# A hybrid decoder block on one core: attention units at a shorter lane period, scan-order outputs, the attention norm applied to its outputs, a paced lane for the up operands, and down loads inside the up stage

## The chip, the cores and the metric

One core of a Trainium2 chip runs the whole block. The metric is the device time of one execution in microseconds; the kernel before takes 2269.36 us (median of 3 runs, 2268.54 to 2271.99). In the text, PE is TensorE (matmuls; PEld its weight loads), DVE is VectorE, ACT is ScalarE, POOL is GpSimd and SP is SyncE, whose queue issues most DMAs. An engine executes its own instructions in order; between engines and DMAs, semaphores say what is ready.

## The reference

512 tokens and 16 learned meta tokens, width 2048, all in float32. A state-space mixer and stick-breaking attention share one input projection and one output projection; a gated MLP with a causal convolution follows.

```python
hn = rmsnorm(h, norm_mix_g)
proj = hn @ w_in                                  # 2048 -> 1024 (u) + 3 * 1024 (q, k, v)
u = proj[..., :1024]; q, k, v = split(proj[..., 1024:], 3)
y_ssm = s5_mixer(u, ...)                          # 64 groups: diagonal complex scan over time,
                                                  # gelu, then y * sigmoid(y @ w_glu + b_glu)
y_attn = stick_breaking_attention(q, k, v)        # 16 heads of 64
mixed = concat([rmsnorm(y_ssm, g_ssm_out), rmsnorm(y_attn, g_attn_out)])
h = h + mixed @ w_out
hn = rmsnorm(h, norm_ffn_g)
gate, val = split(causal_depthwise_conv(hn @ w_up, conv_w, conv_b), 2)      # 5632 each
h = h + (silu(gate) * val) @ w_down
out = rmsnorm(h, norm_final_g)[:, 16:]

# stick breaking, per head:
log_keep = where(kpos < qpos, log_sigmoid(-z), 0)
w = where(kpos < qpos, exp(log_sigmoid(z) + cumsum_from_the_right(log_keep) - log_keep), 0)
y = w @ v
```

## The kernel before

Everything is kept transposed: features on the 128 partitions, the 528 (later 514) positions along the free axis. A float32 product is three matmuls: each operand is split into a high part, rounded to the matmul's format (a cast on ACT), and the low rest (a subtraction on DVE), and `mm3` (L317 to L319) adds high x high, high x low and low x high into one PSUM bank. Weights are split the same way as they stream in: `fetch` (L188, L195) issues the load on SP into one of three raw buffers, L239 casts on ACT (tiles `wh`), `sub` (L114) makes the rest on DVE (`wl`), about two blocks ahead of their use. The helpers `mul`, `add` and `sub` have the lines L108, L111 and L114, ACT's `act` L102.

`dense` runs one output tile of 128 features: for each block of 8 k-tiles and each half of the positions 24 matmuls, then the evacuation of the half's bank. Banks come from three pools: three `d`, three `z` (lanes), two `y`. While both lanes exist, `dbank` takes two of every five banks from `y`.

Work that isn't dense runs in lanes, Python generators that are advanced by the stream of dense matmuls. `pulse` adds 1.4 ns per column of each k-step to a credit, and each time the credit reaches `period` one lane step is written into the program at that place. So the order is fixed when the program is built. The scan lane comes first (period 1600), for eight chunks of 128 channels: `ssm_prep` builds a chunk's tables, `ssm_main` loads the chunk from `udram` (L711), multiplies, scans and stores to `ydram`. Then the attention lane (period `PERATT`), four units of four heads: a unit loads k, q, v (`s<-qkv`, L832), splits them, transposes v (L871, L874), and then puts out 12 items, one every two steps. Each item passes stage a (scores on PE, L914 to L930, exponentials and logarithm on ACT), stage a2 (suffix sums on DVE, L952 to L955), stage b (transposes L982, exponential) and stage c (times v, L1028 and, for the last 16 queries, L997), 2, 4 and 6 steps after a. `hold` stops the lanes, `drain` runs what is left of them without dense work in between.

The stages: three u tiles together (`banks`, six banks, emptied at the first L108 operations after the norm factor, L361 to L377), five more u tiles, 24 tiles of k, v and q, eight gate tiles (`w_glu`, lanes held), the output projection's 16 tiles over the state-space half (`out_part(y2, ...)`), `drain`, its 16 tiles over the attention half (`out_part(ya, ...)`), the up stage, the down stage, the final norm.

The state-space outputs come back from `ydram` with time split as four phases of 132; `ready_y` puts them into the order of time while splitting them (L1181 on ACT, L114 on DVE). The attention half's products are multiplied by the norm factor when they leave the bank, added to h on POOL, squared on ACT for the next norm, stored (`hres`) and scaled by the up stage's gain (`x_scaled`, L1297).

The up stage multiplies by a Strassen-like scheme: seven products (`PROD`) per pair of blocks, whose operands are sums and differences of the halves of `xg[p]` and `xg[p + 8]`. `x_part` makes one operand and splits it: sum on DVE, cast on ACT (L1318), rest on DVE (L114). For p = 0 to 4 (`EARLY`) all seven are made after the tile that completes the pair, for p = 5 to 7 in the first up block. `gated` computes the convolution, silu and product of one block in `later` steps inside the next block and stores it (`fact`); the down stage loads these again and splits them (`load_f`, `split_f`, L396), the first six after the up stage's end.

## Time and profile before

| | |
|---|---|
| median of 3 runs | 2269.36 us (2268.54 to 2271.99) |
| profiled execution | 2271.95 us, span 2270.2 us |
| mean granted TensorE clock | 0.979 |
| loads and stores | 335 MB at a mean of 148 GB/s |

The profile page gives, for each engine, busy time, share of the span and count of instructions. A row of waits reads: engine, tile and line that waited, `<-` what ended the wait, then total us, times and the longest. A row of groups reads: line, engine, operation, tiles out `<-` in, shapes, count, then busy us, mean ns of one, then the idle time of that engine ahead of them. Tile names are those of the program without numbers (`d`, `z`, `y` banks; `s` the common pool of 67 tiles; `at` attention scores; `rstd` a norm factor).

The stages in the profile, from the start: opening u tiles to 53 us; u tiles to 116; k, v, q to 524; gate to 573; output projection's state-space half to about 712, then the drain, and from about 730 its attention half; up stage 850 to 1756; down stage to 2257; final norm.

### The profile page before, as it was taken

How to read it: one execution, taken by the hardware profiler on the slowest of the kernel's cores; microseconds unless marked ns; L12 is line 12 of the kernel's file. 1: busy time of each engine (PE TensorE's matmuls, PEld its weight loads, DVE VectorE, ACT ScalarE, POOL GpSimd, SP SyncE). 2: the span in 40 equal slices, each digit the busy share in tenths (PEclk: the TensorE clock that was granted, in tenths of full speed). 3: DMA queues.
4: the chain of work that ended last, by engine and by line, in shares of the span. 5: the costliest groups of instructions: out<-in, count | busy, mean ns of one | idle time of the engine just before them, and what ended most of it. 6: DMA issues, size and time to landing. Idle time of an engine off the chain costs nothing.

```text
span 2270.2 us, 39806 instructions
## 1 busy us (share of the span) xinstructions
PE 2189.7 (96%) x16196; PEld 2071.2 (91%) x16196; DVE 1576.9 (69%) x2385; ACT 1045.9 (46%) x1668; POOL 251.7 (11%) x370
## 2 busy tenths in 40 slices
PE   7999999999998889999999999999999999999997
PEld 7999998998898888999999999999999788888887
DVE  7877776666777658777887778877787544444464
ACT  5154453565665445555455554555544222222235
POOL 0000000001221350101111011111110000000004
PEclk9999999999999998999999999999999999999999
DMA  5323234242333245777777777777775533333342
GB/s 210 112 93 105 95 99 137 95 123 80 117 123 101 91 144 150 195 194 200 195 195 192 195 201 194 195 195 192 201 194 159 202 122 121 116 119 118 112 148 75
DMA packets 118808, 335.11 MB, mean 148 GB/s; under 512 B 13025, under 2 KB 25697, under 8 KB 118625
## 3 DMA queue, kind: packets, MB, share of 16 engines
q1 hardware_dynamic: 100288, 269.56, 36.6%
q0 software_dynamic: 17472, 61.89, 13.2%
q8 instruction: 127, 2.08, 0.4%
q10 hardware_dynamic: 864, 1.11, 0.2%
q14 instruction: 57, 0.46, 0.1%
HBM read 300.23 MB, written 32.28 MB: 146 GB/s over the span
## 4 chain that ended last, share of the span: by engine, by line
PE 83%; DVE 7%; ACT 4%; issue 2%; DMA 2%; POOL 1%; SPq 0%; DVEq 0%; ACTq 0%; POOLq 0%
PE d L318 20%; PE d L317 19%; PE d L319 19%; PE z L318 4%; PE z L317 4%; PE z L319 4%; PE y L318 3%; PE y L317 3%; PE y L319 3%; DVE s L108 2%; DVE s L114 2%; DVE wl L114 1%; DMA s<-udram 1%; PE z L930 1%; ACT wh L239 1%
## 5 line engine op out<-in xcount | busy, mean ns | idle before, releaser
L317 PE MATMUL d<-s,wh 128*128 128x258 f32 (+4 forms) x3376 | 1047.0, 310 | 35.4 <-DVE s L108 17.0
L318 PE MATMUL d<-s,wh 128*128 128x258 f32 (+4 forms) x3376 | 1042.7, 309 | 7.2 <-DVE s L114 4.4
L319 PE MATMUL d<-s,wl 128*128 128x258 f32 (+4 forms) x3376 | 1036.1, 307 | 0.0
L317 PEld LDWEIGHTS d<-s,wh 128*128 128x128 f32 x3376 | 647.5, 192 | 67.3 <-DVE s L108 13.2
L318 PEld LDWEIGHTS d<-s,wh 128*128 128x128 f32 x3376 | 649.7, 192 | 39.5 <-DVE s L114 8.9
L319 PEld LDWEIGHTS d<-s,wl 128*128 128x128 f32 x3376 | 650.7, 193 | 27.7 <-DVE wl L114 0.2
L239 ACT CAST wh<-wr 128x1024 fp32r<-128x1024 f32 (+2 forms) x209 | 197.5, 945 | 420.5 <-PE d L318 327.0
L114 DVE TENSOR_TENSOR wl<-wr,wh 128x1024 fp32r<-128x1024 f32 (+2 forms) x209 | 235.5, 1127 | 106.8 <-ACT wh L239 106.5
L111 DVE TENSOR_TENSOR s<-s,d 128x512 f32<-128x512 f32 (+1 forms) x144 | 90.5, 629 | 261.6 <-PE d L319 256.5
L317 PE MATMUL z<-s,wh 128*128 128x258 f32 (+1 forms) x752 | 214.9, 286 | 2.4 <-ACT s L1318 2.4
L318 PE MATMUL z<-s,wh 128*128 128x258 f32 (+1 forms) x752 | 216.1, 287 | 0.0
L319 PE MATMUL z<-s,wl 128*128 128x258 f32 (+1 forms) x752 | 213.0, 283 | 0.0
L111 POOL TENSOR_TENSOR s<-s,s 128x514 f32<-128x514 f32 (+1 forms) x89 | 108.4, 1218 | 769.7 <-ACT s L102 653.3
L317 PE MATMUL y<-s,wh 128*128 128x258 f32 (+1 forms) x640 | 183.0, 286 | 0.0
L318 PE MATMUL y<-s,wh 128*128 128x258 f32 (+1 forms) x640 | 182.5, 285 | 0.0
L319 PE MATMUL y<-s,wl 128*128 128x258 f32 (+1 forms) x640 | 182.1, 285 | 0.0
L114 DVE TENSOR_TENSOR wl<-wu,wh 128x1024 fp32r<-128x1024 f32 x132 | 162.1, 1228 | 1.8 <-ACT wh L239 1.3
L239 ACT CAST wh<-wu 128x1024 fp32r<-128x1024 f32 x132 | 138.9, 1052 | 34.2 <-ACT s L102 32.6
L317 PEld LDWEIGHTS z<-s,wh 128*128 128x128 f32 x752 | 143.1, 190 | 3.3 <-ACT s L1318 3.2
L319 PEld LDWEIGHTS z<-s,wl 128*128 128x128 f32 x752 | 144.6, 192 | 0.0
L318 PEld LDWEIGHTS z<-s,wh 128*128 128x128 f32 x752 | 143.8, 191 | 0.6 <-DVE s L114 0.5
L114 DVE TENSOR_TENSOR wl<-wu_s,wh 128x1024 fp32r<-128x1024 f32 x88 | 108.3, 1230 | 38.6 <-ACT wh L239 38.6
(222 smaller groups left out, 2903.6 us busy)
## 6 DMA issues: line engine op xcount, KB each, us to landing
wu<-w_up SPq DMA_DIRECT2D x132, 512.0 KB, 5.1
wu_s<-w_up SPq DMA_DIRECT2D x88, 512.0 KB, 4.6
wu_s<-w_up POOLq DMA_DIRECT2D x88, 512.0 KB, 6.8
wr<-w_down SPq DMA_DIRECT2D x96, 384.0 KB, 3.0
wr<-w_in SPq DMA_DIRECT2D x63, 512.0 KB, 4.1
wr<-w_out SPq DMA_DIRECT2D x32, 512.0 KB, 3.9
fact<-s POOLq DMA_DIRECT2D x44, 256.0 KB, 2.7
s<-fact SPq DMA_DIRECT2D x44, 256.0 KB, 3.4
```

What stands on the lines that cost most here:

```text
L108: e.tensor_tensor(out, a, b, op=ALU.mult)
L111: e.tensor_tensor(out, a, b, op=ALU.add)
L114: e.tensor_tensor(out, a, b, op=ALU.subtract)
L239: S.copy(hi[:, r], raw[:, r])
L317: PE.matmul(ps, whi, xhi, start=start, stop=False, **kw)
L318: PE.matmul(ps, whi, xlo, start=False, stop=False, **kw)
L319: PE.matmul(ps, wlo, xhi, start=False, stop=stop, **kw)
L930: PE.matmul(zs[0][:, x, :], qq[:, i, r], kk[:, :k], start=False, stop=x == nh - 1 and i_ == 2, skip_group_check=True,)
```

## The change

- The scan lane loads chunk j + 1 when chunk j's inputs are no longer needed, ahead of chunk j's outputs; the second table of `ssm_prep` is built earlier and the generator has one step less. The counter that picks a dense tile's bank starts at 2 in place of 0.
- `PERATT` goes from 1350 to 1100. A unit's loads are issued while the unit before is still at its last items, or four steps ahead for the first; v's two tiles are transposed in two steps; the squares of a unit's outputs and their store move two steps behind the last stage c. The lane is also held under the last query tile.
- The gate multiplies in the order of the scan: `ready_y` splits without reordering, and the gate's product is written into the order of time.
- The attention lane ends with the norm factor of the attention outputs, multiplies the eight tiles by it and splits them. The products of the attention half are added to h straight from the bank on DVE.
- A lane with period 1100 makes one up operand per step, its subtraction one step behind its cast. In the first up block the casts for the next product are made between the matmuls of the current one; the norm of the up stage is spread over its steps.
- The first six `fact` tiles and the first six `hres` tiles are loaded, and those of `fact` split, inside the last up block; its own gated product is computed under the first down tiles.

```diff
 PERIOD = 1600.0
-PERATT = 1350.0
+PERATT = 1100.0
+PERX = 1100.0
...
-        turn = [0]
+        turn = [2]
...
+        def split_high(x, g, n):
+            hi, lo = slot([P, n], F32R), slot([P, n], F32R)
+            S.mul(hi, x, g)
+            return (hi, lo), (lo, x, g, hi)
+        def split_low(lo, x, g, hi):
+            V.scalar_tensor_tensor(lo, x, g, hi.bitcast(F32), op0=ALU.mult, op1=ALU.subtract)
...
+        def chunks_in(j):
+            if j not in loaded:
+                loaded[j] = slot([P, 4, NC4])
+                nc.sync.dma_start(loaded[j], udram[j].rearrange("s x q c -> (s x) q c"))
+            return loaded[j]
...
+            del loaded[j]
+            if uready[0] > j + 1:
+                chunks_in(j + 1)
             Y = slot([P, 4, NC4])
...
+                for n, it in enumerate(un.items):
+                    if n > 5 and nxt is None and u < 3 and qkv_ready[0] > u + 1:
+                        nxt = Unit(u + 1)
+                        nxt.loads()
                     un.stage_a(it)
...
-            for j in (6, 7, 0, 1, 2, 3, 4, 5):
-                ya[j] = split(yatt[j], vcol(V_GATT, j), LT)
-                if j % 2:
-                    yield
+            yield from tick(2)
+            rs = rstd_tile()
+            yield from rms_steps(rs, acc_a.pop(), HT, 1024)
+            last = None
+            for j in (6, 7, 0, 1, 2, 3, 4, 5):
+                yield
+                mul(V, yatt[j], yatt[j], rs[:, :LT])
+                if last:
+                    split_low(*last)
+                ya[j], last = split_high(yatt[j], vcol(V_GATT, j), LT)
+            split_low(*last)
...
-                    S.copy(hi.rearrange("p (c t) -> p t c", t=4), yraw[j])
...
+                    S.copy(hi, yraw[j])
+                    sub(V, lo, yraw[j], hi.bitcast(F32))
...
+                    hold[0] = (un, what, p) == (3, QT, 1)
                     dense(xg, hf, evac, ready_y if (un, what, p) == (3, QT, 1) else None)
...
+        def x_lane():
+            period[0] = PERX
+            for p in range(EARLY):
+                while p + 8 not in xg:
+                    yield
+                last = None
+                for n in PROD:
+                    x = x_hi(p, n)
+                    if last:
+                        x_lo(*last)
+                    last = x
+                    yield
+                x_lo(*last)
+                del xg[p], xg[p + 8]
+                yield
...
-        out_part(ya, acc_a.pop(), att_done, ORD)
...
+        lanes.append([x_lane()])
+        for o in ORD:
+            dense(ya, HT, lambda ps, a, b: add(V, h[o][:, a:b], h[o][:, a:b], ps))
+            x = h[o]
+            x_scaled(o)
+            if o < KT - 1:
+                acc_square(accf, o == 0, x, LT)
+        hlast = x
+        drain()
...
+                    if f == 0 and i < 6 and j == 2:
+                        xs = [x_hi(p, PROD[i + 1]) for p in range(EARLY, 8)]
+                    if f == 0 and i < 6 and j == 4:
+                        for y in xs:
+                            x_lo(*y)
+                        next(norm, None)
...
+                if f == NF - 1:
+                    if i == 0:
+                        for x in range(6):
+                            load_f(x)
+                    elif i < 4:
+                        split_f(2 * i - 2)
+                        split_f(2 * i - 1)
+                    elif i < 6:
+                        for x in range(3 * i - 12, 3 * i - 9):
+                            load_h(x)
...
-        later(99)
-        for f in range(6):
-            load_f(f)
-        for f in range(6):
-            split_f(f)
```

What this does to the order, at three places. First PE at the end of the opening stage, where the last matmuls into the six opening banks are followed by the first ordinary u tile (number 681; `s` is the input, `wh` the high weights). Before:

```order
L317 MATMUL z_153<-s_348,wh_445 128x264
L318 MATMUL z_153<-s_349,wh_445 128x264
L319 MATMUL z_153<-s_348,wl_447 128x264
L317 MATMUL d_681<-s_134,wh_517 128x264
L318 MATMUL d_681<-s_135,wh_517 128x264
```

Now:

```order
L318 MATMUL z_153<-s_348,wh_445 128x264
L319 MATMUL z_153<-s_349,wh_445 128x264
L320 MATMUL z_153<-s_348,wl_447 128x264
L318 MATMUL y_681<-s_134,wh_517 128x264
L319 MATMUL y_681<-s_135,wh_517 128x264
```

The tile's bank is a `y` in place of a `d`, and the three `d` banks are the opening tiles'.

Second, DVE at the end of the state-space half of the output projection, from the evacuation of its last tile's second half (`s_8731`, now `s_8841`) on. `s_8102` and `s_8103`, now `s_8079` and `s_8080`, are the last unit's attention outputs; the others with `vec` are outputs loaded back. Before:

```order
L108 TENSOR_TENSOR s_8731<-d_8733,rstd_6876 128x256
L1035 COPY s_8102<-y_8774 128x128
L1035 COPY s_8103<-y_8774 128x128
L1002 COPY s_8102<-y_8868 128x16
L1002 COPY s_8103<-y_8868 128x16
L400 SCALAR_TENSOR_TENSOR s_8910<-s_8102,vec,s_8909 128x514
L400 SCALAR_TENSOR_TENSOR s_8914<-s_8103,vec,s_8913 128x514
L400 SCALAR_TENSOR_TENSOR s_8918<-s_8897,vec,s_8917 128x514
```

Now:

```order
L109 TENSOR_TENSOR s_8841<-d_8843,rstd_6868 128x256
L374 SCALAR_TENSOR_TENSOR s_8898<-s_8896 128x258
L374 SCALAR_TENSOR_TENSOR s_8899<-s_8897 128x256
L109 TENSOR_TENSOR s_8898<-s_8898,s_8894 128x258
L109 TENSOR_TENSOR s_8899<-s_8899,s_8895 128x256
L379 SCALAR_TENSOR_TENSOR rstd_8893<-s_8898,s_8896 128x258
L379 SCALAR_TENSOR_TENSOR rstd_8893<-s_8899,s_8897 128x256
L109 TENSOR_TENSOR s_8079<-s_8079,rstd_8893 128x514
L109 TENSOR_TENSOR s_8080<-s_8080,rstd_8893 128x514
L400 SCALAR_TENSOR_TENSOR s_8934<-s_8079,vec,s_8933 128x514
L109 TENSOR_TENSOR s_8701<-s_8701,rstd_8893 128x514
L400 SCALAR_TENSOR_TENSOR s_8939<-s_8080,vec,s_8938 128x514
```

The copies of the last attention outputs are gone from behind the last evacuation (they stand ahead of it now), and the second part of the norm and the multiplications by its factor have come in ahead of and between the splits.

Third, DVE in the attention half. Before, from the evacuation that completes the pair p = 0 (`rstd` is the norm factor; `s<-s` at 258 wide are sums and rests of up operands):

```order
L108 TENSOR_TENSOR s_9090<-d_9092,rstd_8947 128x256
L114 TENSOR_TENSOR s_9161<-s_9152,s_9161 128x258
L114 TENSOR_TENSOR s_9164<-s_9152 128x258
L114 TENSOR_TENSOR s_9166<-s_9164,s_9166 128x258
L1311 SCALAR_TENSOR_TENSOR s_9169<-s_9164,s_9159 128x258
L114 TENSOR_TENSOR s_9171<-s_9169,s_9171 128x258
L114 TENSOR_TENSOR s_9174<-s_9159,s_9174 128x258
L114 TENSOR_TENSOR s_9177<-s_9159,s_9152 128x258
L114 TENSOR_TENSOR s_9179<-s_9177,s_9179 128x258
L114 TENSOR_TENSOR s_9182<-s_9159,s_9182 128x258
```

Now, two tiles later, with L112 the addition to h straight from the bank and L115 the subtractions:

```order
L112 TENSOR_TENSOR s_6991<-s_6991,d_9106 128x258
L1325 SCALAR_TENSOR_TENSOR s_9152<-s_9128,s_9101 128x258
L115 TENSOR_TENSOR s_9130<-s_9128,s_9130 128x258
L115 TENSOR_TENSOR s_9154<-s_9152,s_9154 128x258
L112 TENSOR_TENSOR s_6991<-s_6991,d_9107 128x256
L115 TENSOR_TENSOR s_9190<-s_9101,s_9039 128x258
L115 TENSOR_TENSOR s_9166<-s_9101,s_9166 128x258
L115 TENSOR_TENSOR s_9192<-s_9190,s_9192 128x258
```

The evacuations now stand between the operands of one pair, and a rest stands behind the next operand's sum.

## The prediction

> **What bounds the kernel now.** I read the page first, then who TensorE waited for, then busy time and clock by stretches.

> ```profile
> span 2270.2 us, 39806 instructions
> ...
> PE 2189.7 (96%) x16196; PEld 2071.2 (91%) x16196; DVE 1576.9 (69%) x2385; ACT 1045.9 (46%) x1668; POOL 251.7 (11%) x370
> ```

> TensorE (PE) is busy for 96% of the span, and the change leaves its matmuls as they are. So only two things can be won: idle time of PE, and matmuls that run at a lower clock. The waits of PE (line waited for: total us, times, longest):

> ```profile
> PE d L317 <- DVE s L108: 17.0, 6, 5.0
> PE z L737 <- DMA s<-udram: 5.6, 6, 1.4
> PE d L317 <- ACT s L396: 5.4, 1, 5.4
> PE d L317 <- ACT wh L239: 5.3, 1, 5.3
> PE d L318 <- DVE s L114: 4.4, 4, 1.9
> PE z L874 <- ACT s L872: 3.6, 3, 2.6
> PE z L914 <- DVE at L114: 3.6, 2, 3.2
> PE d L317 <- ACT s L399: 3.4, 1, 3.4
> ...
> ```

> Busy time by stretches (start:end, length, busy us and matmuls of PE, weight loads, DVE, ACT, POOL, then PE's granted clock):

> ```profile
> 36.00:62.00 26.00, 18.16 (x129) 17.64 (x128) 22.95 (x61) 9.38 (x14) 3.62 (x7) 0.87 0.51 156
> 137.00:382.00 245.00, 238.44 (x1978) 235.36 (x1977) 185.51 (x324) 109.24 (x220) 7.39 (x41) 1.00 0.32 103
> 382.00:403.00 21.00, 17.67 (x127) 16.26 (x126) 7.64 (x17) 12.02 (x26) 0.00 (x0) 0.84 0.45 153
> 497.00:530.00 33.00, 29.20 (x200) 25.55 (x199) 22.72 (x28) 21.92 (x31) 0.00 (x0) 0.84 0.50 146
> 622.00:702.00 80.00, 79.26 (x697) 73.37 (x696) 62.28 (x101) 48.59 (x92) 20.40 (x31) 1.00 0.34 109
> 712.00:736.00 24.00, 17.18 (x163) 15.82 (x162) 17.12 (x26) 12.83 (x23) 5.47 (x4) 0.79 0.36 124
> 760.00:850.00 90.00, 76.38 (x573) 75.10 (x571) 52.05 (x89) 41.07 (x74) 47.15 (x41) 0.91 0.41 126
> 820.00:830.00 10.00, 7.20 (x49) 6.98 (x48) 5.69 (x11) 6.19 (x10) 5.52 (x5) 0.83 0.44 131
> 850.00:905.00 55.00, 50.09 (x323) 45.77 (x324) 43.80 (x74) 28.76 (x51) 6.07 (x8) 0.88 0.55 142
> 1000.00:1100.00 100.00, 100.00 (x831) 100.00 (x830) 80.51 (x99) 51.56 (x70) 11.69 (x15) 1.00 0.74 197
> 1750.00:1772.00 22.00, 14.98 (x79) 12.75 (x78) 14.78 (x24) 8.77 (x14) 1.14 (x2) 0.77 0.69 239
> ```

> From 1000 to 1100 us PE runs without a gap: 831 matmuls in 100 us, 0.120 us each. In the other rows the loss is the idle time plus length times (1 - clock), or, where all matmuls are of that kind, length minus count times 0.120. A dip of the clock always stands beside a wait. Each part of the change aims at one of these rows.

> **Step by step.** Each gain is set against that row's loss.

> *First bank.* The first tile behind the opening stage now writes a y bank, so it needn't wait for DVE to empty the d banks (the 5.0 us under L108). Row 36:62 loses 7.8 idle and 0.13 x 26 = 3.4 by clock. Of that, 5.0 + 3.4 = 8.4 at most is this wait. DVE, though, is busy for 22.95 of the 26 us and has to work through its parameter steps before the first scan chunk: a PE that is early there waits for it later. I take 2.5, between 0 and 8.4, nearer to 0 because of that row.

> *Scan chunks* are fetched one chunk ahead: 5.6 us of waits on udram, on a clock of 1.00. One step less before each chunk's start may bring back about half a microsecond. I take 6, between 0 (another lane operand is late instead) and 6.6, the stretch's whole idle time.

> *First attention unit.* It loads four steps before it uses the loads, and the transposes of v are spread over two steps; before, four banks were asked of a pool of three (L874, 3.6 us). Row 382:403 loses 3.3 idle + 0.16 x 21 = 3.4. I take 5.5, between 2 (ACT's work alone is late) and 6.7.

> *Outputs in scan order* and a held lane under the last query tile: row 497:530 loses 3.8 + 0.16 x 33 = 9.1. The durations (mean ns behind the busy time):

> ```profile
> L111 POOL TENSOR_TENSOR s<-s,s 128x514 f32<-128x514 f32 x61 | 86.7, 1422 | 300.5 <-ACT s L102 184.1 <-DMA s<-xT 52.0 <-DVE s L108 38.6
> ...
> L108 DVE TENSOR_TENSOR s<-s,rstd 128x514 f32<-128x514 f32 x48 | 32.9, 690 | 0.1
> ...
> L1181 ACT CAST s<-s 128x528 fp32r<-128x528 f32 x8 | 8.1, 1171 | 0.0
> ...
> L400 DVE SCALAR_TENSOR_TENSOR s<-s,vec,s 128x514 fp32r<-128x514 f32 x8 | 6.4, 872 | 1.8 <-ACT s L399 1.8
> ...
> L396 ACT CAST s<-s 128x528 fp32r<-128x528 f32 x8 | 4.8, 635 | 6.5 <-DMA s<-qkv 6.4
> ```

> The eight permuted casts of 1171 ns become plain ones, like the 635 of L396, and the lane's work no longer stands between. ACT then needs 5.1 us instead of 9.4, in the second half of a tile of 96 x 0.120 = 11.5 us; DVE's subtractions shrink alike. The last of them still end a little behind the tile, about 1.5 us of waiting. I take 7.5, between 4 and 9. The gate's own operations keep their sizes: nothing. The hold moves lane steps from that tile into the output projection, where the shorter period makes room.

> *Shorter period.* A lane step comes after 1.10 us of dense work instead of 1.35. DVE is busy for 62.28 of 80 us, 78%, while units run. If all of that stretch were scaled by 1.35/1.10 it would be 96%; PE's own lane matmuls don't shrink, so I take 85%. Each stage then has less time until the next one needs it. Against this stand the waits at the front of units (L914, 3.6 us), which the early loads remove. I take -1, between +4 and -20 (half a weight split of 1.29 us in each of some 33 items; 11 full items a unit, three units).

> *Norm factor in the attention outputs.* This moves a chain ahead of the attention half: sum of squares, the norm's steps, then for each of eight tiles a multiplication and a split. By the order of instructions the lane's last attention matmul now stands some 60 dense matmuls ahead of the attention half, the norm's two matmuls 12 ahead, and the multiplications and splits behind the last one: drained with PE waiting. Before, the drain held the last unit's end and eight splits. The norm's chain, from the first norm of the program:

> ```profile
> 44.19 1.16 PE L361 MATMUL y<-s,consts 128*128 128x264 f32 x4 [2.88 <-DVE s L111]
> ...
> 47.68 0.77 DVE L377 SCALAR_TENSOR_TENSOR rstd<-s,s 128x264 f32<-128x264 f32 x2
> ```

> That is 4.3 us until the factor is there. Then DVE needs 8 x 0.690 + 8 x 0.872 = 12.5 us. PE hides 12 x 0.120 = 1.4 of it, and works off 24 matmuls, 2.9, as tiles come. So 12.5 us idle; two POOL additions of 1.42 us ahead of the norm, behind another tile's, add some 2; the clock's dip some 3.5. That is 18, against 6.8 + 0.21 x 24 = 11.8 at most in row 712:736 (about 10.6, as the two overlap). I take -7, between 0 and -13.

> *Attention half.* Row 760:850: 90 - 573 x 0.120 = 21.1 us lost, though DVE is busy for 52 of 90. Its groups there:

> ```profile
> L114 DVE TENSOR_TENSOR s<-s,s 128x258 fp32r<-128x258 f32 x35 | 14.9, 448 | 14.2 <-ACT s L1318 14.2
> L114 DVE TENSOR_TENSOR wl<-wr,wh 128x1024 fp32r<-128x1024 f32 x11 | 14.2, 1293 | 4.0 <-ACT wh L239 4.0
> L114 DVE TENSOR_TENSOR s<-s 128x258 f32<-128x258 f32 x5 | 8.8, 1759 | 0.0
> ```

> After every second tile seven up operands are made in one go: DVE stands idle 14.2 us for ACT's casts, and the next tile's evacuation stands behind. The third row has subtractions of 1759 ns at a size that takes 448 above, while POOL is busy for 47 of 90 us. Now one operand is made per step, its cast a step ahead of the subtraction, and 16 of POOL's additions go; DVE adds straight from the bank instead of multiplying (32 of one size for 32). For a pair of tiles, 96 x 0.120 = 11.5 us, DVE needs at most 2 x 1.29 + 11 x 0.448 + 1.76 + 4 x 0.45 = 11.1, and less with a freer POOL. I take 19.5, between 12 and 21.1.

> *First up block.* Row 850:905: 55 - 323 x 0.120 = 16.2 us lost. Casts now stand ahead of subtractions. But the work is not less: 33 operations of 0.45, seven weight splits of 1.29, two sums of about 1.22 and some four microseconds of norm and evacuation are about 30 us of DVE in 168 x 0.120 = 20.2 of PE, of which a lead of one and a half blocks, 4.3, hides a part. The last sum of squares also ends about 4.7 us after the last tile (evacuation 0.4, scaling 0.7, three casts of 0.4, a square of 0.6, POOL's 1.42 and some handing over), and the norm's matmuls now stand 15 matmuls, 1.8 us, behind it: a wait of 2.9. Together 8 to 9 remain. I take 7.5, between 2 and 12.

> Does a wait of 2.9 us cost clock too? Row 820:830 has one of 2.8 (10 - 7.20), and its clock is 0.83: it cost another 1.7 us, which stands in the sum. [...]

> *Early down loads.* Row 1750:1772: 7.0 idle + 0.23 x 22 = 5.1, 10.3 without the overlap. Loads and six splits move into the last up block; DVE, at 80.51 of 100 us, can take 6 x 0.69 = 4.1 more in 20.2, just. ACT may stand for a load while an evacuation waits behind. The last gated block moves under the first down tiles, where PE is the only bound. I take 8.5, between 5 and 10.3.

> **Sum.** 2.5 + 6 + 5.5 + 7.5 - 1 - 7 + 19.5 + 7.5 + 8.5 = 49. The profiled execution took 2271.95 us (1.75 outside its span), which gives 2223; the median of the runs is 2.6 lower, so 2220.5.

> **Rivals.** (1) DVE becomes the bound inside the units: the -20 in place of -1, so 2240. For it: 78% busy now. Against: hardly a wait in 622:702. (2) The paced lane changes little in the attention half, because DVE is the bound there and the 1759 ns subtractions stay; a gain of 5 instead of 19.5 gives 2235. For it: 11.1 of 11.5. Against: 14.2 idle. (3) PE regains nearly all: the first bank 8, the first up block 12, the chain in front of the attention half no longer than before; 2203. (4) Slower: the early loads stand on SyncE's queue ahead of weight loads, and one that waits for a free slot holds them. The weight ring hides about two blocks, 11.5 us; it takes ten such loads that each wait 5 us beyond that, 50 us, to end at 2270 or above. Against: unit loads waited for slots twice, 1.7 us in all (SyncE's queue; same columns as PE's waits):

> ```profile
> SPq L832 <- PE z L982: 1.7, 2, 1.4
> ```

> **Chances.** The forecast with 2204 to 2236 has 0.66, (1) 0.12, (2) 0.10, (3) 0.08, (4) 0.04. The range of 2203 to 2243 takes in the first three and most of the fourth. About 0.2% is what a measurement of this kernel can tell from no change; faster by more 0.94, within it 0.02, slower 0.04.

> **What would show it.** Right: no waits on udram, none of L874; PE without gaps in the attention half; a wait of 12 us or more, with the clock at half, between the two halves of the output projection; a first up block that still loses 6 or more; no gap between up and down. Wrong: waits for DVE's "at" tiles throughout the units, or an evacuation that still stands behind the up operands.

## The result, and the profile after

The changed kernel takes 2241.97 us (median of 4 runs, 2240.49 to 2245.55) against 2270.68 us for the kernel before in the same comparison: a ratio of 0.9876, with a 95% interval of 0.9859 to 0.9894. The forecast was 2220.5 with a range of 2203 to 2243: the sign is right, the time lies at the far edge of the range, and the gain is 29 us of the 49 that the sum gave. The profiled execution took 2240.49 us, 31.5 less than that of before.

The page, span and busy times of the changed kernel:

```profile
span 2238.7 us, 39814 instructions
...
PE 2170.9 (97%) x16196; PEld 2057.8 (92%) x16196; DVE 1574.1 (70%) x2395; ACT 1042.1 (47%) x1664; POOL 227.6 (10%) x354
```

The matmuls are the same 16196; what has changed is who they wait for. The waits of PE, the longest first:

```profile
PE z L735 <- ACT s L103: 16.1, 6, 6.0
PE d L318 <- ACT s L396: 7.2, 1, 7.2
PE d L319 <- DVE s L115: 6.4, 7, 2.7
PE z L735 <- ACT s L704: 6.4, 2, 5.7
PE d L318 <- ACT wh L240: 5.4, 1, 5.4
PE z L937 <- DVE at L115: 4.0, 2, 3.0
PE y L363 <- POOL s L112: 3.5, 2, 2.4
```

L735 is the first instruction of a scan chunk (before, L717), and it waits 22.5 us in all. Before, the same instruction waited 2.8 us in all; the larger part of that was

```profile
PE z L717 <- ACT s L686: 2.2, 2, 1.1
```

L396 is the first split of the attention outputs, L363 the norm's matmul. The waits on `udram`, for the opening banks, for v's transposes and for the down stage's first splits are gone. The same in stretches (columns as before):

```profile
36.00:62.00 26.00, 24.65 (x200) 24.30 (x199) 23.92 (x68) 9.22 (x14) 3.63 (x7) 1.00 0.50 147
104.00:126.00 22.00, 15.62 (x104) 15.06 (x103) 13.89 (x28) 8.81 (x20) 0.10 (x1) 0.77 0.27 73
126.00:200.00 74.00, 63.12 (x499) 62.26 (x498) 48.47 (x86) 32.04 (x64) 0.53 (x5) 0.93 0.27 87
388.00:405.00 17.00, 17.00 (x147) 16.66 (x146) 9.93 (x20) 10.54 (x24) 0.00 (x0) 1.00 0.62 220
513.00:533.00 20.00, 18.96 (x148) 18.12 (x148) 12.98 (x19) 12.46 (x19) 1.36 (x1) 1.00 0.51 158
716.00:738.00 22.00, 11.97 (x51) 9.78 (x51) 16.43 (x27) 8.34 (x14) 2.65 (x3) 0.71 0.11 37
738.00:828.00 90.00, 88.53 (x730) 88.03 (x730) 58.81 (x100) 44.60 (x80) 27.53 (x30) 1.00 0.44 146
828.00:870.00 42.00, 34.26 (x251) 33.32 (x250) 34.51 (x64) 23.12 (x45) 5.35 (x6) 0.92 0.50 132
1718.00:1742.00 24.00, 24.00 (x171) 22.63 (x170) 19.49 (x28) 12.98 (x20) 0.58 (x1) 1.00 0.60 206
```

The first row has no idle opening any more, the fourth no idle first unit, the seventh is an attention half with 730 matmuls in 90 us where there were 573, the last a change to the down stage without a gap. Against that, rows two and three (the first scan chunks) lose 17 us to idle time and up to 10 more to the clock (0.23 x 22 + 0.07 x 74), and the sixth is the drain. In the kernel before, whose scan starts some 8 us later, the first chunks lost 5 us to idle time:

```profile
112.00:131.00 19.00, 15.96 (x110) 15.41 (x110) 13.47 (x27) 9.69 (x20) 0.00 (x0) 0.84 0.30 85
131.00:200.00 69.00, 66.70 (x550) 65.51 (x550) 50.27 (x91) 33.97 (x71) 0.74 (x7) 1.00 0.28 93
```

To set each stage against its forecast, the table gives its loss: over all matmuls of PE, the time from a start to the next start, less the median of that time for the same shape in the profile of before. Stages are cut at the same number of dense matmuls, so they hold the same dense work.

| Stage (dense matmuls) | before | changed | gain | forecast (bounds) |
|---|---|---|---|---|
| opening and u tiles (to 768) | 13.3 | 4.9 | +8.4 | +2.5 (0 to 8.4) |
| scan (to 2400) | 17.5 | 33.2 | -15.7 | +6 (0 to 6.6) |
| first attention unit (to 2500) | 6.5 | 0.2 | +6.3 | +5.5 (2 to 6.7) |
| units beside k, v, q (to 3072) | 3.1 | 3.7 | -0.6 | -1 (-20 to +4), with the row after next |
| gate, scan-order outputs (to 3456) | 8.5 | 3.0 | +5.5 | +7.5 (4 to 9) |
| units beside the state-space half (to 4224) | 11.3 | 10.8 | +0.5 | see above |
| drain (to 4260) | 10.2 | 14.6 | -4.4 | -7 (-13 to 0) |
| attention half (to 4992) | 19.3 | 1.8 | +17.5 | +19.5 (12 to 21.1) |
| first up block (to 5500) | 17.5 | 11.7 | +5.8 | +7.5 (2 to 12) |
| change to the down stage | 10.3 | 0.1 | +10.2 | +8.5 (5 to 10.3) |
| all the rest | 3.1 | 5.0 | -1.9 | 0 |
| sum | 120.6 | 89.0 | +31.6 | +49 |

One row left its bounds: the scan, 21.7 us away from its forecast. The first bank, 5.9 us better than taken, pays some of it back; the others together make up 1.6 us of loss.

### The profile page after: what moved, and what is told of

Same layout as the page of the kernel before. It is cut to its first block, busy times and chain, and to the rows that moved or that the text cites. A ratio compares the mean times of both kernels' runs of the same rounds, so it can differ in the third digit from the quotient of the medians.

```text
span 2238.7 us, 39814 instructions
## 1 busy us (share of the span) xinstructions
PE 2170.9 (97%) x16196; PEld 2057.8 (92%) x16196; DVE 1574.1 (70%) x2395; ACT 1042.1 (47%) x1664; POOL 227.6 (10%) x354
## 4 chain that ended last, share of the span: by engine, by line
PE 80%; DVE 4%; ACT 2%; issue 2%; DMA 0%; POOL 0%; DVEq 0%; ACTq 0%; POOLq 0%
PE d L319 19%; PE d L318 19%; PE d L320 19%; PE z L319 4%; PE z L318 4%; PE z L320 4%; PE y L319 2%; PE y L318 2%; PE y L320 2%; PE z L953 1%; DVE wl L115 1%; PE z L1005 1%; PE y L1044 1%; DVE s L115 1%; DVE s L109 1%
## 5 line engine op out<-in xcount | busy, mean ns | idle before, releaser
L318 PE MATMUL d<-s,wh 128*128 128x258 f32 (+4 forms) x3376 | 1038.7, 308 | 14.1 <-ACT s L396 7.2
L318 PEld LDWEIGHTS d<-s,wh 128*128 128x128 f32 x3376 | 639.0, 189 | 43.9 <-ACT s L396 7.5
L319 PEld LDWEIGHTS d<-s,wh 128*128 128x128 f32 x3376 | 642.1, 190 | 39.5 <-DVE s L115 7.9
L320 PEld LDWEIGHTS d<-s,wl 128*128 128x128 f32 x3376 | 642.8, 190 | 28.3 <-DVE wl L115 0.2
L240 ACT CAST wh<-wr 128x1024 fp32r<-128x1024 f32 (+2 forms) x209 | 197.5, 945 | 396.7 <-PE d L319 327.6
L115 DVE TENSOR_TENSOR wl<-wr,wh 128x1024 fp32r<-128x1024 f32 (+2 forms) x209 | 233.3, 1116 | 120.7 <-ACT wh L240 109.6
L112 DVE TENSOR_TENSOR s<-s,d 128x512 f32<-128x512 f32 (+2 forms) x176 | 103.4, 589 | 265.0 <-PE d L320 262.4
L318 PE MATMUL z<-s,wh 128*128 128x258 f32 (+1 forms) x752 | 214.1, 285 | 0.0
L318 PE MATMUL y<-s,wh 128*128 128x258 f32 (+1 forms) x640 | 182.9, 286 | 0.0
L115 DVE TENSOR_TENSOR wl<-wu,wh 128x1024 fp32r<-128x1024 f32 x132 | 161.4, 1223 | 5.8 <-ACT wh L240 5.6
L240 ACT CAST wh<-wu 128x1024 fp32r<-128x1024 f32 x132 | 138.9, 1053 | 32.7 <-ACT s L103 32.7
L112 POOL TENSOR_TENSOR s<-s,s 128x514 f32<-128x514 f32 (+1 forms) x73 | 83.3, 1144 | 683.0 <-ACT s L103 545.8
L318 PEld LDWEIGHTS z<-s,wh 128*128 128x128 f32 x752 | 142.4, 189 | 0.0
L115 DVE TENSOR_TENSOR wl<-wu_s,wh 128x1024 fp32r<-128x1024 f32 x88 | 107.9, 1226 | 41.4 <-ACT wh L240 41.4
```

Source lines behind the costliest of these rows:

```text
L112: e.tensor_tensor(out, a, b, op=ALU.add)
L115: e.tensor_tensor(out, a, b, op=ALU.subtract)
L240: S.copy(hi[:, r], raw[:, r])
L318: PE.matmul(ps, whi, xhi, start=start, stop=False, **kw)
L319: PE.matmul(ps, whi, xlo, start=False, stop=False, **kw)
L320: PE.matmul(ps, wlo, xhi, start=False, stop=stop, **kw)
```

## The experiments

Each kernel is the changed one with the edit shown. Medians are of 4 to 7 runs; the kernel before took 2269.66 to 2270.5 us beside them. A stage's loss comes from one profiled execution, and one that the edit can't touch still differs by up to 3 us (the opening in x4 and in e1). The losses by stage in one table ("units" are the rows to 3072 and to 4224 of the table above, the first unit with them):

| Kernel | median us | opening | scan | units | gate | units | drain | att. half | first up |
|---|---|---|---|---|---|---|---|---|---|
| before | 2270.68 | 13.3 | 17.5 | 9.6 | 8.5 | 11.3 | 10.2 | 19.3 | 17.5 |
| changed | 2241.97 | 4.9 | 33.2 | 3.9 | 3.0 | 10.8 | 14.6 | 1.8 | 11.7 |
| e1 old table order | 2228.00 | 4.3 | 12.6 | 8.9 | 1.8 | 18.8 | 13.9 | 3.1 | 11.7 |
| e2 counter at 0 | 2249.96 | 14.1 | 31.9 | 3.9 | 2.5 | 13.4 | 13.9 | 1.8 | 13.2 |
| e3 PERATT 950 | 2251.48 | 4.5 | 34.1 | 7.2 | 6.5 | 30.4 | 0.0 | 2.3 | 11.7 |
| e4 additions on POOL | 2258.90 | 4.7 | 33.8 | 3.9 | 3.3 | 10.8 | 14.5 | 16.6 | 15.6 |
| e5 no pace | 2249.76 | 4.7 | 33.4 | 3.9 | 2.5 | 13.4 | 13.9 | 9.2 | 11.8 |
| e6 norm later | 2243.16 | 4.5 | 33.6 | 3.9 | 2.6 | 13.3 | 13.9 | 1.8 | 13.3 |
| e7 seven pairs | 2241.64 | 5.1 | 32.8 | 3.9 | 2.4 | 10.8 | 14.6 | 3.7 | 10.7 |
| e8 no hold at the gate | 2246.55 | 4.5 | 13.1 | 4.2 | 35.1 | 17.2 | 0.0 | 1.2 | 11.9 |
| x1 up part | 2240.14 | 4.4 | 33.2 | 3.9 | 3.4 | 11.2 | 14.5 | 3.3 | 10.8 |
| x2 scan at 1450 | 2234.50 | 4.6 | 36.9 | 5.1 | 4.2 | 4.8 | 7.9 | 5.1 | 10.6 |
| x3 scan at 1400 | 2262.81 | 5.0 | 53.9 | 5.8 | 1.3 | 18.6 | 7.2 | 4.7 | 10.4 |
| x4 old order, shifted | 2221.00 | 7.3 | 13.1 | 3.8 | 4.4 | 11.0 | 14.5 | 2.0 | 11.7 |

### e1: the scan's tables in the old order

```diff
-            cplx(1, kk, [rep(t) for t in sp["c"]], HB[1])
             for c in range(2):
                 cplx(c, rr, [rep(t) for t in sp["bbar"]], PB[c])
                 ...
-                if c == 0:
-                    yield
+                yield
+            cplx(1, kk, [rep(t) for t in sp["c"]], HB[1])
```

> The changed kernel with one piece undone: the order and the number of steps in which the next scan chunk's tables are built. From the end of the u tiles to the first attention unit the changed kernel loses 33 us against TensorE's steady pace, the kernel before 17.5. Theory A (order): the second transposed table is finished in the very step ahead of the transposes, six products and eight ACT copies at once, and a weight cast is caught behind them on ACT; with the old order the loss falls to 12 to 17 us and the time to 2222 to 2227 us. Theory B (DVE is full until the second chunk, and TensorE merely came to it 8 us earlier because of the first bank): the waits come back at other places, the loss stays at 25 or more, and the time at 2234 us or above.

2228.0 us, 14 less than the changed kernel; the scan loses 12.6 us in place of 33.2. That is what theory A said of the scan; the time is a little above its window, since the units lose more than in the changed kernel (x4, below). With the waits on `udram` gone, the scan is also 4.9 us better than before.

e1 takes back two things together, the order of the tables and the one step less. What they do is seen in ACT's timeline of the changed kernel ahead of the second chunk (start, length, then the idle time before and what ended it):

```profile
148.75 0.82 ACT L704 COPY s<-x 64x256 f32<-64x256 f32 x2 [11.05 <-DVE x L106]
149.94 0.83 ACT L704 COPY s<-x 64x256 f32<-64x256 f32 x2 [0.37 <-DVE x L106]
150.80 0.85 ACT L103 ACTIVATE s<-s 64x256 f32<-64x256 f32 x2
151.68 1.05 ACT L240 CAST wh<-wr 128x1024 fp32r<-128x1024 f32 x1
155.15 0.82 ACT L704 COPY s<-x 64x256 f32<-64x256 f32 x2 [2.42 <-DVE x L106]
155.98 0.84 ACT L103 ACTIVATE s<-s 64x256 f32<-64x256 f32 x2
156.83 1.28 ACT L103 ACT_TABLE_LOAD   x1
158.13 0.67 ACT L103 ACTIVATE s<-z 128x264 f32<-128x264 f32 x2
```

and in DVE's at the same time:

```profile
149.42 0.43 DVE L106 TENSOR_TENSOR x<-x,x 128x256 f32<-128x256 f32 x1
152.76 1.22 DVE L115 TENSOR_TENSOR wl<-wr,wh 128x1024 fp32r<-128x1024 f32 x1 [2.91 <-ACT wh L240]
153.90 0.75 DVE L109 TENSOR_TENSOR x<-AR,s 128x256 f32<-128x256 f32 x2
154.69 0.42 DVE L106 TENSOR_TENSOR x<-x,x 128x256 f32<-128x256 f32 x1
```

ACT stands 11.05 us for DVE's products (`x`), while a weight cast (L240) queues behind the copies. When the cast comes, DVE has stood 2.91 us for it, since its weight split (`wl`) is next in its own queue; the last products are behind that split, ACT's last copies behind them, and behind those the table load and the activation at 158.13, which empties a `z` bank of the chunk's outputs. PE's transposes want that bank: they are there at 152.6 and wait until 158.57. DVE and ACT, each in order, wait for each other in turn: none of it is work that they hadn't done before. In e1 the eight copies for the two transposed tables come in one piece, with no cast and no split between:

```profile
145.38 0.82 ACT L704 COPY s<-x 64x256 f32<-64x256 f32 x2 [5.92 <-DVE x L106]
146.22 0.84 ACT L103 ACTIVATE s<-s 64x256 f32<-64x256 f32 x2
147.07 0.82 ACT L704 COPY s<-x 64x256 f32<-64x256 f32 x2
147.91 0.84 ACT L103 ACTIVATE s<-s 64x256 f32<-64x256 f32 x2
```

PE's waits of this run in the scan (100 to 370 us) are then:

```profile
PE z L734 <- ACT s L704: 3.1, 2, 2.5
PE z L754 <- ACT s L103: 2.0, 3, 0.9
PE z L734 <- ACT s L103: 0.6, 1, 0.6
```

Is it the order, or the place of the cast? The traces point to the place. In the changed kernel the weight cast stands between the copies of the two transposed tables ahead of chunks two to six, and the transposes there wait 6.0, 4.8, 1.3, 1.7 and 1.8 us. Ahead of chunks seven and eight the order of the tables is the same, but the cast stands in front of them all, and the waits are none and 0.4 us. x3 (below) has the old order: where its other period puts a cast between the two, ahead of chunks three, five and seven, the transposes wait 3.9, 3.2 and 3.7 us, and ahead of four, six and eight, where none stands there, they don't wait (ahead of two they wait 2.6 us without one, so the place is not all). The one step less may well be what moved the cast: ahead of chunks two to eight the transposes stand 12 to 18 dense matmuls earlier in the changed kernel than in e1. The two pieces weren't run apart. The first chunk, which waits 5.75 us for 2.54 in e1, has no cast between; there the products of the table that was moved forward stand ahead of those that the transposes need.

### e2: the bank counter at 0

```diff
-        turn = [2]
+        turn = [0]
```

> The changed kernel with the bank counter at 0 again, so that the first u tile waits for the opening banks. Theory A (the waits at the scan chunks come from the order of the tables alone): the opening loses its 8.4 us again and nothing is given back: 2250 us. Theory B (DVE sets when the first chunks can start): what the opening loses, the first chunk's wait of 5.8 us and its lowered clock give back: 2240 to 2244 us, no change.

2249.96 us: the opening loses 14.1 us again, and the scan gives back only 1.3 of it (31.9 for 33.2). Theory A. The lane's steps are placed by dense matmuls, so a PE that comes later shifts the chain as well; the waits ahead of chunks two to eight are the same to 0.01 us.

### e3: PERATT at 950

```diff
-PERATT = 1100.0
+PERATT = 950.0
```

> The changed kernel with PERATT at 950 in place of 1100, nothing else. Theory A (the chain of norm factor, multiplications and splits is exposed only because the lane's last steps find no dense work left): some 20 more lane steps fit ahead of the drain, its loss falls from 14.6 us to 2 to 5, and the time to 2230 to 2233 us. Theory B (DVE becomes the bound inside the units at this period): waits of TensorE for the scores' suffix sums appear in all four units, together 10 us or more, and the time is 2240 us or above.

2251.48 us. Both mechanisms are seen, and the second is larger: the drain loses nothing any more (14.6 before), but the units beside the state-space half lose 30.4 us for 10.8. The waits of PE in this run:

```profile
PE z L937 <- DVE at L115: 7.5, 4, 4.9
PE z L893 <- ACT at L103: 4.1, 1, 4.1
PE z L1005 <- DVE at L115: 2.7, 5, 1.4
PE z L995 <- DVE at L115: 2.7, 2, 2.2
```

All of these wait for one item's stages on DVE and ACT, for the most part beside the state-space half, and a clock of 0.95 from 577 to 747 us comes on top: rival (1) of the prediction, at 950 and not at 1100.

### e4 and e5: POOL and the pace in the attention half

e4 puts the additions to h on POOL again:

```diff
-            dense(ya, HT, lambda ps, a, b: add(V, h[o][:, a:b], h[o][:, a:b], ps))
+            t = slot([P, LT])
+            dense(ya, HT, lambda ps, a, b: V.tensor_copy(t[:, a:b], ps))
+            add(G, h[o], h[o], t)
+            t = None
```

> The changed kernel with the attention half's additions to h on POOL again (DVE copies the bank, POOL adds the whole tile), the up operands still made one per step. Theory A (what mattered in the attention half is the pace, since DVE stood behind ACT's casts): the half still loses 2 to 5 us, and the time is 2242 to 2246 us. Theory B (what mattered is POOL's work beside DVE, which had stretched subtractions of 448 ns to 1759): operations of DVE that meet an addition take 1.5 us or more again, TensorE waits for them, the half loses 8 to 15 us, and the time is 2248 to 2256 us.

e5 makes the seven operands of a pair in one step:

```diff
                     last = x
-                    yield
                 x_lo(*last)
```

> The changed kernel with all seven up operands of a pair made in one lane step again; the casts still stand one ahead of the subtractions, and DVE still adds straight from the bank. Theory A (the pace matters: seven casts and rests in a row hold up the next tile's addition and the next weight split): the attention half loses 8 us or more in place of 1.8, and the time is 2248 us or above. Theory B (POOL's additions between a bank and its consumers were what mattered, the pace was not): the half loses at most 4 us, and the time is 2240 to 2245 us.

e4: 2258.9 us, the half loses 16.6 and the first up block 3.9 more than in the changed kernel; theory B by its numbers, and by more than expected. e5: 2249.76 us, the half loses 9.2; theory A. So both parts of the edit were needed, and the larger is POOL's. PE's largest waits in the half, of e4 and of e5:

```profile
PE d L318 <- DVE s L1366: 13.0, 8, 2.4
```

```profile
PE d L318 <- DVE s L112: 8.3, 5, 1.9
```

In both PE waits for a bank that DVE hasn't emptied. In e4 the way there is a queue: ACT's scaling of a tile (L1312) waits for POOL, and the casts of operands and weights stand behind it (ACT's waits from 740 us on, e4 and then the changed kernel):

```profile
ACT s L1312 <- POOL s L112: 50.1, 15, 7.7
```

```profile
ACT s L1312 <- DVE s L112: 24.9, 14, 3.6
```

DVE in turn waits 37 us for casts in the half, where it waits 26 in the changed kernel. Theory B's own reason, operations of DVE that take longer beside an addition on POOL, is there as well but is the smaller change: counted over 419 ns for 128x258 and 1222 ns for a weight split, it costs DVE about 15 us in e4's half, and about 11 in the changed kernel's and in that of before. How much of the 14.8 us each of the two makes was not separated.

### e6, e7 and x1: the first up block

e6 puts the norm's two matmuls nine matmuls later in the first product; e7 makes seven pairs of operands in the lane in place of five:

```diff
-                        next(norm, None)
+                        if i:
+                            next(norm, None)
+                    if f == 0 and i == 0 and j == 7:
+                        next(norm, None)
```

```diff
-        EARLY = 5
+        EARLY = 7
```

> The changed kernel with the two matmuls of the up stage's norm nine matmuls (1.1 us) later in the first product. Theory A (they come too early for the last sum of squares, and the wait of 2.4 us brings the lowered clock with it): the wait shrinks to about 1.3 us, the clock stays up there, the first up block loses 8 to 9.5 us in place of 11.6, and the time is 2239 to 2240 us. Theory B (DVE is what the first block waits for in any case): the next products wait longer by as much, 2242 us.

> The changed kernel with the operands of seven pairs made in the lane under the attention half in place of five, so that the first up block makes those of one pair in place of three. Theory A (DVE has room in the half, 77% busy, and none in the first block): the first block loses 3 to 6 us in place of 11.6, the half no more than 4, and the time is 2233 to 2238 us. Theory B (the half has no room left, since every operation that is held up there is stood behind in order): the half loses 8 us or more, and the time is 2242 us or above.

e6: 2243.16 us, no gain. The norm's wait falls from 2.4 to 0.9 us, and the waits for rests in the block rise from 5.4 to 7.3. Theory B. e7: 2241.64 us, no change either, and neither theory as it stood: the half holds (3.7), the waits for rests in the first block, 5.4 us, are gone, but the block still loses 10.7, because the norm's matmul now waits 8.0:

```profile
PE y L363 <- POOL s L112: 9.2, 2, 8.0
```

x1 takes e6 and e7 together and puts the square of h's last tile ahead of the drain:

```diff
-            if o < KT - 1:
-                acc_square(accf, o == 0, x, LT)
-        hlast = x
+            acc_square(accf, o == 0, x, LT)
         drain()
...
-                    acc_square(accf, False, hlast, LT)
```

> The changed kernel with seven pairs of up operands made in the lane, the square of h's last tile put ahead of the drain of that lane, and the norm's matmuls nine matmuls later in the first product. Theory A (with seven pairs alone the first block lost as much as before only because the norm's two matmuls then waited 8.0 us for a sum of squares that stands behind the drained operands): that wait falls below 2 us, the first block loses 3 to 5 us in place of 11.6, and the time is 2233 to 2237 us. Theory B (the operands drained behind the last tile are themselves what the first block waits for): the loss moves to the first product's operands, and the time is 2240 us or above.

2240.14 us, the block loses 10.8. Theory B: the first product's operands are late by almost as much.

```profile
PE d L318 <- ACT s L1335: 5.8, 1, 5.8
```

Three other orders of the same work give 10.7 to 13.3 us, for 11.7. The last tile of h is needed before the block can run, so the share of operands made early isn't what it waits for in the end. In x1 the 5.8 us are the way of that tile: PE stops at 833.8 us, DVE empties the tile's first half at 836.90, behind a lane operand's rest and a weight split that had stood for its cast, the scaling starts at 838.02 and the cast that PE wants at 839.17. So the queue ahead of the tile counts as much as the chain behind it; neither was shortened alone.

### e8: no hold at the gate

Old table order, PERATT at 1250, and

```diff
         y2 = []
-        hold[0] = True
+        hold[0] = False
```

> The changed kernel with the old order of the scan's tables, the lanes not held under the gate's eight tiles, and PERATT at 1250: the lane then gets 384 more dense matmuls to run beside, and by the order of instructions its norm stands some 200 matmuls ahead of the attention half, in spite of the longer period. Theory A (what bounds the units is DVE's work per time, and DVE is only 62% busy in the gate's stage): the scan loses 13 us in place of 33, the units 8 to 12 in all as in the changed kernel, the drain at most 3 in place of 14.6; the time is 2207 to 2214 us. Theory B (the gate's own chains of sigmoid, product and split can't stand beside the lane's): the gate's stage loses 10 us or more, and the time is 2220 us or above.

2246.55 us. The scan and the drain do as theory A says, but the units lose 21.4 us in all, not 8 to 12, and the gate's stage 35.1. That is theory B by its numbers; the reason is neither theory's. ACT is busy for 97.43 of 107 us there, and its two largest groups are:

```profile
L103 ACT ACT_TABLE_LOAD x15 | 19.2, 1283 | 0.3
L99 ACT ACT_TABLE_LOAD x14 | 18.0, 1283 | 0.3
```

The gate's sigmoids and the scores' exponentials alternate on ACT here, and 29 table loads of 1283 ns stand among them, 37 us. In the changed kernel, with the lane held, there is one in this stage, of 1283 ns.

### x2 and x3: a shorter period for the scan

```diff
-PERIOD = 1600.0
-PERATT = 1100.0
+PERIOD = 1450.0        # x3: 1400.0
+PERATT = 1150.0        # x3: 1200.0
```

with the old table order and the up part of x1.

> The old order of the scan's tables, the scan's period at 1450 in place of 1600, PERATT at 1150, and the up part of the run with seven pairs. By the order of instructions the attention lane starts some 140 dense matmuls earlier and its norm stands 138 ahead of the attention half, in spite of the longer period. Theory A (the drain can be filled by time taken from the scan, where DVE is 76% busy and waits are few with the old order): the scan loses 13 to 18 us, the units 8 to 18, the drain at most 3, the first up block 3 to 5; the time is 2200 to 2215 us. Theory B (DVE has no more room in either lane, and each step that comes earlier is waited for): scan and units together lose 45 us or more, and the time is 2222 us or above.

> As the run before it, with the scan's period at 1400 and PERATT at 1200: the same end of the lane, but more of the time taken from the scan. Theory A (the units' waits fall with their period, and the scan has the room): units lose 3 to 5 us less than in the run before it, the scan at most 3 more; 2198 to 2215 us. Theory B (the scan is at its limit already): the scan loses 8 us or more beyond the run before it, and the time is above that run's.

x2 takes 2234.5 us, x3 2262.81. Theory B for the scan in both: at 1600 it loses 12.6, at 1450 36.9, at 1400 53.9. The first row is x2's, the second x3's (PE's waits in the scan):

```profile
PE z L734 <- ACT s L704: 8.2, 2, 7.6
```

```profile
PE z L734 <- ACT s L103: 13.7, 5, 3.9
```

In x2 the largest wait, 7.6 us, is the first chunk's. In x3 three of the five in its row are those where a cast stands between the tables (e1), so part of its loss is place and not room on DVE. The drain does shrink, to 7 or 8 us, not to the 3 that theory A named.

### x4: the old order, with the units where they were

```diff
             for _ in ahead:
                 pass
-            yield
+            if j < 7:
+                yield
```

on top of e1.

> The old order of the scan's tables, as in the first of these runs, and one lane step less at the scan's end, nothing else. From the first attention unit on, every lane instruction then stands at the same dense matmul as in the changed kernel; with the old order alone all of them stood 10 to 18 matmuls later, and the units and the drain lost 43 us in place of 32. Theory A (what the old order gave back in the units was this shift: with a lane so close to DVE's limit, it matters which lane step falls beside which evacuation and weight split): units and drain lose 32 us as in the changed kernel, the scan 13, and the time is 2219 to 2224 us. Theory B (it was the order itself, TensorE coming to the units 20 us earlier while the weights or DVE's backlog don't): units and drain lose 40 us or more again, and the time stays at 2227 us or above.

2221.0 us (2220.16 to 2224.08), a ratio to before of 0.9782 (0.9769 to 0.9795): theory A, and the fastest kernel here, 21 us below the changed one. The units, the gate and the drain lose 33.7 us, where e1, with the same instructions 10 to 18 dense matmuls later, lost 43.4.

```profile
span 2221.2 us, 39801 instructions
...
PE 2167.6 (98%) x16196; PEld 2054.9 (93%) x16196; DVE 1575.2 (71%) x2395; ACT 1041.1 (47%) x1664; POOL 227.6 (10%) x354
```

## Why the prediction was right and where it was wrong

*Scan chunks* (+6, measured -15.7): this step failed. It priced the prefetch and passed over the other edit in the same lines, the tables' order, with "One step less before each chunk's start may bring back about half a microsecond". The prefetch itself was sized about right: with it and the old order and steps (e1), the scan gains 4.9. But the chain from DVE's products over ACT's copies to the transposes had to be followed against the weight casts and splits that the dense work puts between; with one of these between the two tables, a chunk waits 1.3 to 6.0 us. The row that was priced, 137 to 382 us, also leaves out the first chunk, which now waits 6.4. And the lower bound, 0, let another operand be late only by what the prefetch saves; a loss was not thought of. With the scan at its measured size the sum would have been 27, and with the first bank's as well 33, within 2 us of the measured 31.6. That the range held the time is luck: it was wide for another reason, rival (1).

*First bank* (+2.5, measured +8.4): mis-sized. I argued that a PE which is early waits for DVE later. e2 shows that it doesn't here: with the counter at 0 the opening loses 9.2 us more, and the time rises by 8.

*Shorter period* (-1, measured -0.1 over both rows of units): right, though nearer to the edge than the forecast saw. At 1100 the units lose what they lost before, at 950 one stage loses 30 us for 11; and one lane step's shift at 1100 costs 10 in these stages and 7 in the time (e1 against x4).

*Norm factor* (-7, measured -4.4): the mechanism was right, a wait for the first split and a clock of 0.51 from 727 to 739 us. But the wait is 7.2 us, not the 12 or more that was named as the sign: the splits of the other tiles came fast enough that PE waited for five of them, 1.6 us in all, and from 716 to 738 us it stood idle for 10.0 us where the sum had 14.5.

*First unit, outputs in scan order, early down loads* (+5.5, +7.5, +8.5; measured +6.3, +5.5, +10.2): as argued. The casts now take 633 ns for the 635 forecast.

*Attention half* (+19.5, measured +17.5): right in size, and e5 shows the reason of the pace. The other reason, fewer of POOL's additions beside DVE, came out otherwise. That subtractions are stretched beside an addition is confirmed: in 738 to 860 us of the changed kernel the 10 sums and subtractions of two 128x258 operands from SBUF that overlap an addition on POOL take 1399 ns on average, the 68 others 419. The 1399 ns are about the length of one addition (1297 ns there). Not all of DVE's operations show it: in the attention half of the kernel before, the 22 multiplications straight from PSUM that overlap an addition take 418 ns, the 6 others 425. But with half the additions (14 for 27) the stretch still costs DVE about 11 us in the half, as before; it fell on more of the subtractions (10 for 8) and on fewer weight splits (4 for 12). So its relief isn't what paid. That more additions on POOL cost so much in e4 goes with the queue on ACT behind them (above), though the two weren't separated.

*First up block* (+7.5, measured +5.8): right, with the wait for the norm at 2.4 us for the 2.9 forecast. That less of DVE's work in the block doesn't help by itself, because the way of the last tile is as long, is what e7 and x1 add.

Of the rivals, (2) and (3) didn't happen (the stretched operations of (2) did stay, but the half gained all the same), and (4) neither: no wait of the up stage is for a weight load. (1) gave about the measured time, 2240, by a mechanism that wasn't at work at 1100.

## What to carry to other kernels

Where a change moves a few small operations between two in-order engines, follow who stands at the head of each queue: an operation that is ready early but queued behind one that waits costs the whole chain, with both engines far from full (ahead of the second chunk of the changed kernel ACT stood 11.05 us for DVE and DVE 2.91 us for ACT, at busy shares of 47% and 70% over the span). A shift of a lane by one step can cost as much as the edit is worth (7 us of time in e1 against x4), since it can put a cast or a split between two links of a chain; so undo the shift before judging the edit. And a term whose bounds leave out a loss needs a reason for it.

## What the runs showed of the hardware

What stays open is how the units' loss depends on their place: 4.8 us at a period of 1150 in x2, 10.8 at 1100, 18.6 at 1200 in x3. No rule for the best place was found.
